# Attention times values: the pair's 128 value columns and a PSUM bank per head, and no clearing product

## The chip, the core and the metric

The kernel runs on one core of a Trainium2 chip. The metric is the device time of one launch in microseconds (us); the median of three runs of the kernel before is 2452.74 us (2452.15 to 2453.5). Engines are named as in the profile: PE (TensorE), DVE (VectorE), ACT (ScalarE), POOL (GpSimd), SP (which issues most of the DMAs).

## The reference, cut to what matters

Two transformer blocks over 512 tokens of 1024 columns, all in float32. Three kinds of attention in them end in a product of a 512 x 512 matrix with 64 value columns for each head:

```
# block 1: softmax attention, 8 MLA heads (masked by chunks of 64) and 8 chunk heads (with a bias)
p = softmax(where(mask, q @ k.T * scale, NEG_INF));            o = p @ v          # v: 512 x 64
# block 2: retention, 8 heads (written with chunks; as one matrix it is causal with decay)
o = (q @ k.T * decay) @ v
# block 2: stick-breaking attention, 8 heads
lneg = where(mask, log_sigmoid(-z), 0); tail = cumsum(lneg, reverse) - lneg
o = where(mask, exp(log_sigmoid(z) + tail), 0) @ v
```

Around them stand dense products (modulation, projections, an MLP) and at the end a mixture of 32 experts, which takes about half of the time.

## The kernel before, in words

All matrices are cut into tiles of 128 rows. A head's attention matrix is held with keys on the partitions and queries along the free dimension, and only the part on and under the diagonal in blocks of 128 is computed: key block `kt` (0 to 3) meets `n = 512 - 128 kt` queries. So a head has four products with its values, of 512, 384, 256 and 128 columns; in each the 128 keys are contracted, the values of that key block are the stationary operand and the attention weights stream. The result is wanted transposed, with the head's 64 value columns on the partitions.

Two heads of even and odd number form a pair. In the kernel before, a pair shares one PSUM bank `po`: the even head's products have its 64 value columns as stationary operand and write partitions 0 to 63, the odd head's write partitions 64 to 127. When both are done, one copy of 128 x 512 takes the bank out. For the softmax and stick-breaking heads the copy is a `split`: ACT writes the rounded part `hh` (line 191) and then DVE the rest `hl` (line 194); for retention it is one ACT copy into `yT` (line 1155).

These operands are plain float32 and not the rounded kind (fp32r) that the dense products use, and every product of float32 operands appears as two MATMULs, each with a weight load of its own.

Three loops issue this work, each as a software pipeline over "units" (head, block), and the order on each engine is the order in which the loop writes it:

- `softmax_attention` (from line 485): step `s` issues the scores of unit `s`, for MLA heads DVE's mask (line 499), the reciprocal of the unit before (line 515), the row maximum (line 501) and ACT's exponential (line 502), for chunk heads DVE's bias and maximum (line 506), the reciprocal, the negation `nm` (line 509) and the exponential (line 510); then DVE's scaling of the unit before (line 520); then, if one is due, the `split` of a finished bank; then the transposes of unit `s - 3` and their copy `pT` (line 562); then the product with the values of unit `s - 9` in `pv`. A split that falls due in step `s` is issued in step `s + 1`, behind the scaling.
- retention in `block2_mix`: scores of unit `s`, DVE's product with the decay into `rw` (line 1141), and the product with the values of unit `s - 3`.
- the stick-breaking loop: scores and a mask product of unit `s`, then Abs, Exp and Ln on ACT (lines 1242 to 1244); DVE turns unit `s - 1` into two parts `sh` and `sl`; PE adds the running sums of unit `s - 3` with the constant matrices in `sc`, and ACT takes the exponential `sw` (line 1268); then the product of unit `s - 5` with the values `vs`.

In the stick-breaking loop a head begins with key block 3, so its first product covers 128 of the 512 columns. A bank is therefore opened by a product with one row of zeros that writes all 128 x 512 elements:

```
if h % 2 == 0 and kt == 3:
    po = self.ps()
    self.mm(po, zero[0:1, :], sc[0:1, 0:4, :].rearrange("p a b -> p (a b)"), True, False)
```

PSUM tiles come from one pool of eight banks.

Of the kernel before, what the change touches and what calls it, by code (L numbers as in the profile page):

```python
# [11 lines left out]
F32R = mybir.dt.float32r  # L12
I32 = mybir.dt.int32
U32 = mybir.dt.uint32
AF = mybir.ActivationFunctionType
OP = mybir.AluOpType
# [113 lines left out]
class Halves:  # L130
    """Eight blocks of columns in two tiles."""

# [8 lines left out]
class Kernel:  # L141
# [36 lines left out]
    def warm(self, n):  # L178
        """Keeps the tensor engine's clock up while it waits for data."""
        if n:  # L180
            ps = self.ps()
            for _ in range(n):
                self.mm(ps[:, 0:P], self.ones, self.ones, True, True)
# [210 lines left out]
    def norm_finish(self, x, xn, ss):  # L394
        """Rows scaled by one over their root mean square."""
        nc = self.nc
        s1 = self.sm.tile([P, NT], F32, name="ns1")
        nc.vector.tensor_tensor(s1, ss[:, :, 0], ss[:, :, 1], op=OP.add)
        r = self.sm.tile([P, NT], F32, name="nr")
        self.rstd(r, s1, D)  # L400
        for t in range(NT):
            if t % 2:
                nc.vector.tensor_scalar(xn[:, t, :], x[:, t, :], r[:, t:t + 1], None, op0=OP.mult)
            else:
                nc.scalar.activation(xn[:, t, :], x[:, t, :], AF.Copy, scale=r[:, t:t + 1])
# [5 lines left out]
    def h_block(self, x, j, scale, bias=None):  # L411
        """One block of columns of x, transposed and scaled, in two parts."""
        nc = self.nc
        ps = self.ps()
        for t in range(NT):
            self.T(ps[:, t * P:(t + 1) * P], x[:, t, j * P:(j + 1) * P])
        if bias is None:
            nc.scalar.activation(self.hh[:, j, :], ps, AF.Copy, scale=scale)  # L418
            nc.vector.scalar_tensor_tensor(self.hl_[:, j, :], ps, scale, self.hh[:, j, :], op0=OP.mult,  # L419
                                           op1=OP.subtract)  # L420
        else:
            tmp = self.junk()
            nc.scalar.activation(tmp, ps, AF.Identity, scale=scale, bias=bias)
            self.split(tmp, self.hh[:, j, :], self.hl_[:, j, :], "dve")

    def h_pair(self, x, j, scale, h, l):
        """As h_block, in tiles of its own."""
        nc = self.nc
        ps = self.ps()
        for t in range(NT):  # L430
            self.T(ps[:, t * P:(t + 1) * P], x[:, t, j * P:(j + 1) * P])
        nc.scalar.activation(h, ps, AF.Copy, scale=scale)
        nc.vector.scalar_tensor_tensor(l, ps, scale, h, op0=OP.mult, op1=OP.subtract)
        return h, l
# [35 lines left out]
    def zeros(self, dst):  # L470
        """Clears what transpose_masked leaves: each head's columns have zeros in the rows of its pair's other one."""
        v = dst.rearrange("p (a b) n -> p a b n", b=2)
        self.nc.gpsimd.memset(v[64:128, :, 0, :], 0.0)
        self.nc.gpsimd.memset(v[0:64, :, 1, :], 0.0)
# [10 lines left out]
    def softmax_attention(self, heads, pool, pool3, tail):  # L485
# [36 lines left out]
        def pv(hd, kt):  # L522
            par = hd["par"]
            if par == 0 and kt == 0:
                self.po = self.ps()
            rows = slice(64 * par, 64 * par + 64)
            self.mm(self.po[rows, kt * P:512], hd["v"](kt), hd["pT"][:, kt, kt * P:512], kt == 0, kt == NT - 1)
            if par == 1 and kt == NT - 1:
                return lambda po=self.po: self.split(po, self.hh[:, hd["pair"], :], self.hl_[:, hd["pair"], :])

# [40 lines left out]
    def block1(self, cg):  # L571
# [19 lines left out]
        with ExitStack() as cx:  # L591
# [44 lines left out]
            def ada(j, m, warm=0):  # L636
                """Columns of the modulation: the first m K tiles on the vector engine."""
                w = wa.pop(j)
# [273 lines left out]
        for h in range(8):  # L912
            heads.append(dict(q=qTm[:, h, :], k=kTm[:, h, :], bias=None, par=h % 2, pair=h // 2,
                              v=lambda kt, h=h: vt[:, kt, h * 64:(h + 1) * 64]))
        for h in range(8):
            heads.append(dict(q=qTc[:, h // 2, :], k=kTc[:, h, :], bias=bias_for(h), par=h % 2,
                              pair=4 + h // 2, v=lambda kt, h=h: vc[:, kt, h * 64:(h + 1) * 64]))
        pso = []
# [122 lines left out]
    def block2_mix(self, right):  # L1041
# [43 lines left out]
        with ExitStack() as cr:  # L1085
# [48 lines left out]
            for s in range(len(units) + la):  # L1134
# [11 lines left out]
                if j >= 0:  # L1146
                    h, kt = units[j]
                    n = 512 - kt * P
                    rows = slice(64 * (h % 2), 64 * (h % 2) + 64)
                    if h % 2 == 0 and kt == 0:  # L1150
                        po = self.ps()
                    self.mm(po[rows, kt * P:512], v[:, kt, h * 64:(h + 1) * 64], wt.pop(j)[:, 0:n], kt == 0,
                            kt == NT - 1)
                    if h % 2 and kt == NT - 1:
                        later = lambda h=h, po=po: nc.scalar.activation(yT[:, h // 2, :], po, AF.Copy)
            later()
# [26 lines left out]
        self.zeros(qTs)  # L1183
        sc = os_.tile([P, 5, P], F32R, name="sc")
        idr, negr, trin, none, zero = [sc[:, i, :] for i in range(5)]
        for i, n in enumerate(("ident", "negm", "trin")):
            nc.vector.tensor_copy(sc[:, i, :], self.cc(n))
        nc.vector.tensor_scalar(none, self.ones, -1.0, None, op0=OP.mult)
        nc.vector.tensor_scalar(zero, self.ones, 0.0, None, op0=OP.mult)
        cs = ExitStack()  # L1190
# [35 lines left out]
        with ExitStack() as cs:  # L1226
# [7 lines left out]
            for s in range(len(units) + la3):  # L1234
# [35 lines left out]
                if 0 <= j < len(units):  # L1270
                    h, kt = units[j]
                    n = 512 - kt * P
                    rows = slice(64 * (h % 2), 64 * (h % 2) + 64)
                    if h % 2 == 0 and kt == 3:
                        po = self.ps()
                        self.mm(po, zero[0:1, :], sc[0:1, 0:4, :].rearrange("p a b -> p (a b)"), True, False)
                    self.mm(po[rows, kt * P:512], vs[:, kt, h * 64:(h + 1) * 64], st.pop(j)[:, 0:n], False, kt == 0)
                    if h % 2 and kt == 0:
                        later[s + 2] = lambda h=h, po=po: self.split(po, self.hh[:, h // 2, :], self.hl_[:, h // 2, :])
        cx.close()  # L1280
# [26 lines left out]
    def router_weights(self):  # L1307
        """Loaded ahead of the router: its weights in two parts and its bias."""
        nc, A, pool = self.nc, self.A, self.big
# [103 lines left out]
    def overflow_blocks(self, rp):  # L1413
        """How many blocks beyond its first each expert has."""
        nc = self.nc
# [5 lines left out]
    def plan(self, rp):  # L1421
        """In steps: which expert's second block shares its weights' pass and the order of the experts that follows
        from it (that expert and TWO change places); the blocks beyond, with their experts, first ranks and places."""
        nc, nb = self.nc, self.nb
# [60 lines left out]
    def swap(self, rp):  # L1485
        """The columns of TWO and of the expert whose second block shares its weights' pass change places."""
        nc = self.nc
# [11 lines left out]
    def gather_onehot(self, d):  # L1499
        """One where a row's number is the token's rank, as the positive part of one less their distance."""  # L1500
        nc = self.nc
# [6 lines left out]
    def gather_table(self, d, a=0, b=2):  # L1508
        """The token (from one) and the gate of each of the block's rows."""
        ps = self.ps()  # L1510
# [6 lines left out]
    def first_rows(self, d, hn):  # L1517
        """The first block's rows, transposed, by products with its one-hot matrix."""
        d["x"] = self.hl_tile("x", d)
# [41 lines left out]
    def m_next(self):  # L1561
        """Parts of the next half chunk (two K tiles); the splits run m_la halves ahead."""
        self.m_ahead()
# [45 lines left out]
    def expert_step(self, cur=(), prev=(), pp=(), nxt=(), extra=None):  # L1609
        """The twelve weight chunks of a step: up products of `cur`'s blocks, down products of `prev`'s, rows of `nxt`'s."""  # L1610
        nc = self.nc
# [112 lines left out]
    def moe_open(self, cx):  # L1724
        """The first expert weights, and the gain of the router's norm."""
        A = self.A
# [14 lines left out]
    def moe_open1(self, cx):  # L1741
        """Ring of expert weights, the biases in two parts and what selects an expert's."""
        nc, A = self.nc, self.A
# [163 lines left out]
    def ple_proj(self, c, pool):  # L1907
        """A half of the columns of p_2 times its projection."""
        ph = self.ph
# [136 lines left out]
```

## Time and profile before

| | |
|---|---|
| median of 3 runs | 2452.74 us |
| span of the profiled execution | 2452.3 us |
| instructions in it | 30624 |
| PE busy | 2419.6 us (99%) |
| DVE busy | 1815.7 us (74%) |
| ACT busy | 1517.4 us (62%) |
| mean granted TensorE clock | 0.991 |

The span runs from the first to the last instruction of one profiled execution. The median of the unprofiled runs lies 0.4 us above it. Busy time of PE counts from the start of a matmul to its modelled end, and matmuls overlap, so 99% does not say that each matmul follows its neighbour at full pace; that is read from start to start. The three attention loops lie at about 170 to 285 us, 797 to 840 us and 915 to 989 us, the experts from about 1180 to 2400 us.

### The profile page before, as it was taken

The page shows a single profiled execution, that of the slowest core. Times are in us where ns is not written, and L with a number is a line of the kernel's source. Part 1 is how long each engine was busy: PE and PEld are TensorE (multiplying, and loading weights), DVE is VectorE, ACT ScalarE, POOL GpSimd, SP SyncE. Part 2 cuts the span into 40 slices and gives each one's busy share as a digit, 9 for nine tenths or more (in the row PEclk, how much of TensorE's full clock was granted, in tenths as well). Part 3 has the DMA queues.
Part 4 walks back from the last instruction along what each step waited for, and adds up shares of the span by engine and source line. Part 5 has one row for each costly group of instructions (what it writes and reads, how often), then busy time and mean ns, then how long its engine had stood idle before and what let it go on. Part 6 is the DMA issues. An engine that isn't in the chain of part 4 may idle for free. (4 is left out here: it accounts for less than half of the span.)

```text
span 2452.3 us, 30624 instructions
## 1 busy us (share of the span) xinstructions
PE 2419.6 (99%) x10796; PEld 1843.8 (75%) x10796; DVE 1815.7 (74%) x2575; ACT 1517.4 (62%) x2201; POOL 164.2 (7%) x108
## 2 busy tenths in 40 slices
PE   8999999999999999989999999999999999999999
PEld 8874688888887475777777777777777777777777
DVE  5876666565556475489888888876888889888874
ACT  3676443334444157467777777855677777777764
POOL 0100000000000000020101010100101010101010
PEclk8999999999999999999999999999999999999999
DMA  9230433342333121579999999877999999999852
GB/s 316 85 126 14 142 105 111 120 121 94 95 113 103 35 68 53 183 259 331 327 335 315 338 321 339 295 254 240 332 337 322 336 321 323 338 326 322 298 190 103
DMA packets 282924, 538.66 MB, mean 220 GB/s; under 512 B 16277, under 2 KB 41397, under 8 KB 282576
## 3 DMA queue, kind: packets, MB, share of 16 engines
q1 hardware_dynamic: 268432, 508.21, 59.6%
q0 software_dynamic: 11792, 26.12, 4.0%
q10 hardware_dynamic: 2544, 2.34, 0.3%
q8 instruction: 86, 1.41, 0.2%
q14 instruction: 70, 0.57, 0.1%
HBM read 530.60 MB, written 23.59 MB: 226 GB/s over the span
## 5 line engine op out<-in xcount | busy, mean ns | idle before, releaser
L194 DVE TENSOR_TENSOR mlo<-mraw,mhi 128x1024 fp32r<-128x1024 f32 x777 | 926.0, 1223 | 181.2 <-ACT mhi L191 173.1
L191 ACT ACTIVATE mhi<-mraw 128x1024 fp32r<-128x1024 f32 x777 | 799.6, 1054 | 203.5 <-PE ps L171 181.6
L171 PE MATMUL ps<-mhi,xh 128*128 128x512 f32 x1024 | 422.7, 413 | 0.0
L171 PE MATMUL ps<-mhi,xl 128*128 128x512 f32 x1024 | 404.4, 395 | 0.0
L171 PE MATMUL ps<-mlo,xh 128*128 128x512 f32 x1024 | 403.6, 394 | 0.0
L171 PEld LDWEIGHTS ps<-mhi,xh 128*128 128x128 f32 x1024 | 192.7, 188 | 67.7 <-issue 30.1
L194 DVE TENSOR_TENSOR wlo<-raw,whi 128x1024 fp32r<-128x1024 f32 (+2 forms) x128 | 152.6, 1203 | 111.2 <-ACT whi L191 110.9
L171 PEld LDWEIGHTS ps<-mhi,xl 128*128 128x128 f32 x1024 | 192.5, 188 | 45.5 <-DVE xl L1596 0.3
L171 PEld LDWEIGHTS ps<-mlo,xh 128*128 128x128 f32 x1024 | 193.1, 189 | 37.3
L191 ACT ACTIVATE whi<-raw 128x1024 fp32r<-128x1024 f32 (+2 forms) x128 | 132.3, 1042 | 131.6 <-PE ps L171 131.2
L171 PE MATMUL ps<-mhi,ah 128*128 128x512 f32 x512 | 211.7, 414 | 0.0
L171 PE MATMUL ps<-mhi,al 128*128 128x512 f32 x512 | 202.3, 395 | 0.0
L171 PE MATMUL ps<-mlo,ah 128*128 128x512 f32 x512 | 202.3, 395 | 0.0
L171 PE MATMUL ps<-whi,hh 128*128 128x512 f32 (+1 forms) x464 | 183.8, 396 | 5.1 <-ACT hh L191 2.4
L171 PE MATMUL ps<-wlo,hh 128*128 128x512 f32 (+1 forms) x464 | 180.8, 390 | 1.9 <-DVE wlo L194 1.9
L171 PE MATMUL ps<-whi,hl 128*128 128x512 f32 (+1 forms) x464 | 180.5, 389 | 0.0
L171 PE MATMUL ps<-hh,whi 128*128 128x512 f32 x352 | 137.8, 392 | 0.0
L171 PE MATMUL ps<-hh,wlo 128*128 128x512 f32 x352 | 137.0, 389 | 0.0
L171 PE MATMUL ps<-hl,whi 128*128 128x512 f32 x352 | 137.0, 389 | 0.0
L1649 ACT ACTIVATE mg<-mg 128x512 f32<-128x512 f32 x66 | 41.7, 632 | 130.2 <-DVE mg L1648 130.2
L171 PEld LDWEIGHTS ps<-mhi,ah 128*128 128x128 f32 x512 | 96.2, 188 | 34.4 <-issue 15.1
L171 PEld LDWEIGHTS ps<-mhi,al 128*128 128x128 f32 x512 | 96.3, 188 | 23.2
(486 smaller groups left out, 3743.1 us busy)
## 6 DMA issues: line engine op xcount, KB each, us to landing
mraw<-in_w_ug SPq DMA_DIRECT2D x256, 1024.0 KB, 6.2
mraw<-in_w_dn SPq DMA_DIRECT2D x128, 1024.0 KB, 6.6
raw<-in_w_up SPq DMA_DIRECT2D x44, 512.0 KB, 3.6
raw<-in_w_in SPq DMA_DIRECT2D x40, 512.0 KB, 3.7
wa<-in_w_ada SPq DMA_DIRECT2D x12, 1024.0 KB, 9.4
raw<-in_w_ada SPq DMA_DIRECT2D x24, 512.0 KB, 4.6
raw<-in_w_down SPq DMA_DIRECT2D x22, 512.0 KB, 3.5
raw<-in_w_out SPq DMA_DIRECT2D x16, 512.0 KB, 4.8
```

The lines of the kernel that those rows point to most:

```text
L171: self.nc.tensor.matmul(out, l, r, start=start, stop=stop, skip_group_check=True)
L191: self.nc.scalar.activation(hi, raw, AF.Copy)
L194: self.nc.vector.tensor_tensor(lo, raw, hi, op=OP.subtract)
L1649: nc.scalar.activation(g, g, AF.Silu, scale=1.702)
```

## The change

All three loops now use the pair's 128 value columns as the stationary operand, for either head. A head's products fill a whole bank of 128 x 512, of which 64 partitions are that head's result and the other 64 are not used; each head has a bank of its own, and only its 64 partitions are copied out, once per head where it was once per pair. In the stick-breaking loop the first product of a head now opens the bank itself, and the product with zeros, its operand and one DVE instruction are gone. Besides, docstrings are emptied, which shifts line numbers by one or two.

```
         def pv(hd, kt):
-            par = hd["par"]
-            if par == 0 and kt == 0:
+            if kt == 0:
                 self.po = self.ps()
-            rows = slice(64 * par, 64 * par + 64)
-            self.mm(self.po[rows, kt * P:512], hd["v"](kt), hd["pT"][:, kt, kt * P:512], kt == 0, kt == NT - 1)
-            if par == 1 and kt == NT - 1:
-                return lambda po=self.po: self.split(po, self.hh[:, hd["pair"], :], self.hl_[:, hd["pair"], :])
+            self.mm(self.po[:, kt * P:512], hd["v"](kt), hd["pT"][:, kt, kt * P:512], kt == 0, kt == NT - 1)
+            if kt == NT - 1:
+                r = slice(64 * hd["par"], 64 * hd["par"] + 64)
+                return lambda po=self.po: self.split(po[r], self.hh[r, hd["pair"], :], self.hl_[r, hd["pair"], :])
...
-                              v=lambda kt, h=h: vt[:, kt, h * 64:(h + 1) * 64]))
+                              v=lambda kt, h=h: vt[:, kt, (h // 2) * P:(h // 2 + 1) * P]))
...
-                    if h % 2 == 0 and kt == 0:
+                    if kt == 0:
                         po = self.ps()
-                    self.mm(po[rows, kt * P:512], v[:, kt, h * 64:(h + 1) * 64], wt.pop(j)[:, 0:n], kt == 0,
+                    self.mm(po[:, kt * P:512], v[:, kt, (h // 2) * P:(h // 2 + 1) * P], wt.pop(j)[:, 0:n], kt == 0,
                             kt == NT - 1)
-                    if h % 2 and kt == NT - 1:
-                        later = lambda h=h, po=po: nc.scalar.activation(yT[:, h // 2, :], po, AF.Copy)
+                    if kt == NT - 1:
+                        later = lambda h=h, po=po, r=r: nc.scalar.activation(yT[r, h // 2, :], po[r], AF.Copy)
...
-                    if h % 2 == 0 and kt == 3:
+                    if kt == 3:
                         po = self.ps()
-                        self.mm(po, zero[0:1, :], sc[0:1, 0:4, :].rearrange("p a b -> p (a b)"), True, False)
-                    self.mm(po[rows, kt * P:512], vs[:, kt, h * 64:(h + 1) * 64], st.pop(j)[:, 0:n], False, kt == 0)
-                    if h % 2 and kt == 0:
-                        later[s + 2] = lambda h=h, po=po: self.split(po, self.hh[:, h // 2, :], self.hl_[:, h // 2, :])
+                    self.mm(po[:, kt * P:512], vs[:, kt, (h // 2) * P:(h // 2 + 1) * P], st.pop(j)[:, 0:n], kt == 3,
+                            kt == 0)
+                    if kt == 0:
+                        later[s + 2] = lambda h=h, po=po, r=r: self.split(po[r], self.hh[r, h // 2, :],
+                                                                          self.hl_[r, h // 2, :])
```

On DVE, in the MLA heads of the softmax loop, these are two steps before (13 and 14, in the fourth head; `nm<-ps` is the row maximum of the step, `prob<-prob,rc` the scaling of the unit before it):

```order
L499 MEMSET ps 64x64
L515 RECIPROCAL rc<-smx 128x1
L501 TENSOR_REDUCE nm<-ps 128x1
L520 TENSOR_SCALAR prob<-prob,rc 128x128
L499 MEMSET ps 64x64
L515 RECIPROCAL rc<-smx 128x1
L501 TENSOR_REDUCE nm<-ps 128x1
L520 TENSOR_SCALAR prob<-prob,rc 128x256
```

And the same steps now:

```order
L499 MEMSET ps 64x64
L515 RECIPROCAL rc<-smx 128x1
L501 TENSOR_REDUCE nm<-ps 128x1
L520 TENSOR_SCALAR prob<-prob,rc 128x128
L194 TENSOR_TENSOR hl<-ps,hh 64x512
L499 MEMSET ps 64x64
L515 RECIPROCAL rc<-smx 128x1
L501 TENSOR_REDUCE nm<-ps 128x1
L520 TENSOR_SCALAR prob<-prob,rc 128x256
```

The subtraction `hl` of a split stands between the scaling of a 128-column unit and the mask of the next step in every head from the fourth on; before, it stood there in every second head, from the fifth on.

On PE, in the stick-breaking loop, this is how the first bank was opened before (`sh`, `sl` with `sc` are the running sums, `sw,vs` the product with the values, `qTs,kTs` the next scores):

```order
L171 MATMUL ps<-sh_7481,sc 128x384
L171 MATMUL ps<-sl_7482,sc 128x384
L171 MATMUL ps<-sc 128x512
L171 MATMUL ps<-sw,vs 64x128
L171 MATMUL ps<-qTs,kTs 128x384
```

And now:

```order
L171 MATMUL ps<-sh_7512,sc 128x384
L171 MATMUL ps<-sl_7513,sc 128x384
L171 MATMUL ps<-sw,vs 128x128
L171 MATMUL ps<-qTs,kTs 128x384
```

The product with zeros is gone, in four places in all, and the products with the values write 128 partitions where they wrote 64; the order of all other products of PE is kept in the three loops.

## Rows read from the trace of the kernel before

**Rows 1.** Stretches: us, then busy PE, PEld, DVE, ACT, POOL, clock, DMA, GB/s
```profile
165.00:181.00 16.00, 12.89 (x58) 8.78 (x57) 8.77 (x36) 11.18 (x31) 1.08 (x2) 0.79 0.36 128
181.00:284.00 103.00, 103.00 (x400) 49.69 (x399) 64.25 (x279) 59.68 (x179) 3.39 (x7) 1.00 0.10 32
...
798.00:838.00 40.00, 40.00 (x114) 13.81 (x113) 13.88 (x29) 1.79 (x3) 0.00 (x0) 1.00 0.00 1
...
939.09:975.29 36.20, 36.20 (x163) 21.40 (x162) 21.46 (x51) 27.77 (x66) 0.00 (x0) 1.00 0.00 1
...
1180.00:2400.00 1220.00, 1217.29 (x5297) 926.79 (x5295) 1032.77 (x1108) 899.59 (x1095) 115.15 (x64) 1.00 0.89 310
```

**Rows 2.** Timeline of PE, one softmax step: start, duration, operation, out<-in, shape, count
```profile
234.31 0.49 PE L187 MATMUL ps<-cst,prob 128*128 128x128 f32 x3
234.73 1.07 PE L171 MATMUL ps<-pT,x 128*64 128x512 f32 x2
235.73 0.91 PE L171 MATMUL ps<-kTc,qTc 128*128 128x384 f32 x2
236.48 0.60 PE L187 MATMUL ps<-cst,prob 128*128 128x128 f32 x4
```

**Rows 3.** Timeline of PE, scores behind transposes without a product with values between
```profile
172.53 0.60 PE L171 MATMUL ps<-kTm,qTm 128*128 128x256 f32 x2
...
172.75 0.38 PE L171 MATMUL ps<-kTm,qTm 128*128 128x256 f32 x1
```

**Rows 4.** Timeline of PE, the last seven products with values of the softmax loop
```profile
281.70 3.12 PE L171 MATMUL ps<-pT,x 128*64 128x384 f32 x14
```

**Rows 5.** Timeline of DVE, an MLA head with a split (square brackets: idle before, releaser)
```profile
194.39 0.41 DVE L501 TENSOR_REDUCE nm<-ps 128x1 f32<-128x256 f32 x1
...
195.97 0.69 DVE L194 TENSOR_TENSOR hl<-ps,hh 128x512 fp32r<-128x512 f32 x1 [0.98 <-ACT hh L191]
...
196.81 0.56 DVE L501 TENSOR_REDUCE nm<-ps 128x1 f32<-128x384 f32 x1
...
198.54 0.69 DVE L501 TENSOR_REDUCE nm<-ps 128x1 f32<-128x512 f32 x1
...
201.16 0.41 DVE L501 TENSOR_REDUCE nm<-ps 128x1 f32<-128x256 f32 x1
```

**Rows 6.** Timeline of ACT in that head: the exponential's sums of the 384-column step
```profile
197.95 0.19 ACT L502 ACTIVATION_READ_ACCUMULATOR prob<-ps,nm 128x1 f32 x1
```

**Rows 7.** Timeline of DVE, a chunk head with a split
```profile
235.08 0.15 DVE L509 TENSOR_SCALAR nm<-mx 128x1 f32<-128x1 f32 x1
...
236.44 0.69 DVE L194 TENSOR_TENSOR hl<-ps,hh 128x512 fp32r<-128x512 f32 x1 [1.00 <-ACT hh L191]
...
237.64 0.15 DVE L509 TENSOR_SCALAR nm<-mx 128x1 f32<-128x1 f32 x1
...
238.96 0.69 DVE L506 CUSTOM_DVE_ANT_0 prob<-ps,relb 128x512 f32<-128x512 f32 x1 [0.89 <-PE ps L171]
...
239.69 0.15 DVE L509 TENSOR_SCALAR nm<-mx 128x1 f32<-128x1 f32 x1
...
240.87 0.14 DVE L509 TENSOR_SCALAR nm<-mx 128x1 f32<-128x1 f32 x1
...
241.85 0.15 DVE L509 TENSOR_SCALAR nm<-mx 128x1 f32<-128x1 f32 x1
```

**Rows 8.** ACT copies of 512 columns from PSUM: duration min/median/max in ns
```profile
L191 ACT ACTIVATE hh<-ps x7: 575/576/606, 195.4 to 280.2; 128x512 fp32r<-128x512 f32 x7
```

**Rows 9.** The same for copies of 64 partitions
```profile
L482 ACT ACTIVATE qT<-ps x8: 590/592/595, 768.7 to 773.0; 64x512 f32<-64x512 f32 x8
```

**Rows 10.** Costliest groups of the page: DVE's part of a weight chunk's split
```profile
L194 DVE TENSOR_TENSOR wlo<-raw,whi 128x1024 fp32r<-128x1024 f32 (+2 forms) x128 | 152.6, 1203 | 111.2 <-ACT whi L191 110.9
```

**Rows 11.** Timeline of PE, the stick-breaking loop around a product with zeros
```profile
940.33 0.49 PE L171 MATMUL ps<-sc 1*128 1x512 f32 x1
940.75 0.43 PE L171 MATMUL ps<-sw,vs 128*64 128x128 f32 x2
```

More of the change, by code (lines that the diff above doesn't have):

```diff
@@ L913, in block1 @@
             heads.append(dict(q=qTm[:, h, :], k=kTm[:, h, :], bias=None, par=h % 2, pair=h // 2,
-                              v=lambda kt, h=h: vt[:, kt, h * 64:(h + 1) * 64]))
+                              v=lambda kt, h=h: vt[:, kt, (h // 2) * P:(h // 2 + 1) * P]))
         for h in range(8):
             heads.append(dict(q=qTc[:, h // 2, :], k=kTc[:, h, :], bias=bias_for(h), par=h % 2,
-                              pair=4 + h // 2, v=lambda kt, h=h: vc[:, kt, h * 64:(h + 1) * 64]))
+                              pair=4 + h // 2, v=lambda kt, h=h: vc[:, kt, (h // 2) * P:(h // 2 + 1) * P]))
         pso = []
@@ L1148, in block2_mix @@
                     n = 512 - kt * P
-                    rows = slice(64 * (h % 2), 64 * (h % 2) + 64)
-                    if h % 2 == 0 and kt == 0:
+                    r = slice(64 * (h % 2), 64 * (h % 2) + 64)
+                    if kt == 0:
                         po = self.ps()
-                    self.mm(po[rows, kt * P:512], v[:, kt, h * 64:(h + 1) * 64], wt.pop(j)[:, 0:n], kt == 0,
+                    self.mm(po[:, kt * P:512], v[:, kt, (h // 2) * P:(h // 2 + 1) * P], wt.pop(j)[:, 0:n], kt == 0,
                             kt == NT - 1)
-                    if h % 2 and kt == NT - 1:
-                        later = lambda h=h, po=po: nc.scalar.activation(yT[:, h // 2, :], po, AF.Copy)
+                    if kt == NT - 1:
+                        later = lambda h=h, po=po, r=r: nc.scalar.activation(yT[r, h // 2, :], po[r], AF.Copy)
             later()
@@ L1183, in block2_mix @@
         self.zeros(qTs)
-        sc = os_.tile([P, 5, P], F32R, name="sc")
-        idr, negr, trin, none, zero = [sc[:, i, :] for i in range(5)]
+        sc = os_.tile([P, 4, P], F32R, name="sc")
+        idr, negr, trin, none = [sc[:, i, :] for i in range(4)]
         for i, n in enumerate(("ident", "negm", "trin")):
@@ L1188, in block2_mix @@
         nc.vector.tensor_scalar(none, self.ones, -1.0, None, op0=OP.mult)
-        nc.vector.tensor_scalar(zero, self.ones, 0.0, None, op0=OP.mult)
         cs = ExitStack()
@@ L1272, in block2_mix @@
                     n = 512 - kt * P
-                    rows = slice(64 * (h % 2), 64 * (h % 2) + 64)
-                    if h % 2 == 0 and kt == 3:
+                    r = slice(64 * (h % 2), 64 * (h % 2) + 64)
+                    if kt == 3:
                         po = self.ps()
-                        self.mm(po, zero[0:1, :], sc[0:1, 0:4, :].rearrange("p a b -> p (a b)"), True, False)
-                    self.mm(po[rows, kt * P:512], vs[:, kt, h * 64:(h + 1) * 64], st.pop(j)[:, 0:n], False, kt == 0)
-                    if h % 2 and kt == 0:
-                        later[s + 2] = lambda h=h, po=po: self.split(po, self.hh[:, h // 2, :], self.hl_[:, h // 2, :])
+                    self.mm(po[:, kt * P:512], vs[:, kt, (h // 2) * P:(h // 2 + 1) * P], st.pop(j)[:, 0:n], kt == 3,
[3 more added lines that the diff above has]
+                                                                          self.hl_[r, h // 2, :])
         cx.close()
```

## The prediction

> **What bounds the kernel now.** I first read the stretches. In the softmax loop PE is busy 103.00 of 103.00 us, in retention 40.00 of 40.00, in four heads of the stick-breaking loop 36.20 of 36.20, while DVE and ACT are busy 4 to 77% of the time; among the experts it is 1217 of 1220 us [rows 1]. So PE sets the end in every stage the change touches, and the experts, also PE's, will simply start earlier by whatever the loops give: their DMA share of 0.89 leaves the loads behind PE, not ahead of it. A busy PE need not be at full pace, however, and that I read next, from start to start.
>
> Three transposes last 0.49 us and four 0.60 [rows 2], so one costs 0.11 at full pace. Scores of 256 columns, which like the products with values are two MATMULs, start 0.22 us apart when transposes stand before them (172.53, 172.75) [rows 3]; so a pass takes 0.22 us per 256 columns, 0.32 for 384, 0.43 for 512. Against this, one softmax step [rows 2]: transposes at 234.31, the product with values at 234.73: 0.42, where three transposes take 0.33. From it to the scores 1.00, where two passes take 0.86. From the scores to the next transposes 0.75, where two passes take 0.64. So each product with 64 value columns costs 0.09 + 0.14 + 0.11 = 0.34 us beyond its columns, around it and in the product behind it. The scores behind transposes in rows 3 do not pay it: it comes with the 64-column shape.
>
> One thing speaks against the change. The last seven products with values of the softmax loop, 14 passes over 4096 columns, run 3.12 us from first start to last end [rows 4]; at the pace above they would need 4096 / 256 x 0.22 = 3.5. Two heads overlap there by some 0.5 us, which the change loses. [...]
>
> **The change part by part.** *The switch.* 64 + 32 + 32 products. The new ones have the same shape of weights as scores and transposes, so I take the 0.34 as gone for each that stands between other shapes. Nothing is added for columns: a pass streams as many as before. The weight load doubles, 128 columns for 64; for scores behind transposes such a load hides in the matmul before [rows 3], and I cost it at nothing; uncovered it would be bounded by the part that the first pass now pays after a switch, 0.1 us.
>
> *Retention.* 28 products lie between scores, four stand together at the end: 28 x 0.34 + 0.3 = 9.8 us; DVE, 13.88 us busy in 40, hides the rest, and four more ACT copies fall on an engine that is busy 1.79 us of 40 [rows 1]. 10 us saved.
>
> *Softmax.* Here PE alone would save 54 x 0.34 + 0.9 - 0.5 = 18.8 us. But half a bank costs the copying engine as much as a whole one: ACT copies of 64 x 512 take 592 ns [rows 9], of 128 x 512 576 [rows 8]. There are 16 splits where there were 8, and a split stands in DVE's queue ahead of the next step's mask, reciprocal and maximum, which the next exponential needs. So I follow the chain DVE, ACT, DVE through a head with a split and leave out where it waits for PE. MLA head, from maximum to maximum [rows 5]: 256 to 384 columns 2.42 us (hl waits 0.98 for hh, then 0.69); 384 to 512 is 1.73 with a wait for PE; without it ACT's sums are ready at 197.95 + 0.19 = 198.14 [rows 6], and 0.1 later the maximum could start, so 1.44; 512 over 128 to 256 2.62. Sum 6.48. The head takes 201.16 - 194.39 = 6.77 now, and PE after the change 6.77 - 4 x 0.34 = 5.4. So the chain takes PE's place: an MLA head saves 0.29, not 1.36. Chunk head, from nm to nm [rows 7]: 2.56 with the split, 2.05 less the 0.89 of waiting for PE, 1.18, 0.98: 5.88; it saves 0.89. The loop has steps 9 to 63 with products behind them: 9 to 12 without a split save PE's 1.4; the other 4.75 MLA heads 1.4; eight chunk heads 7.1; the tail, with PE alone, 0.9 - 0.5. From this goes one weight chunk that DVE splits near the end and that PE's lag now covers: its DVE part is 1.2 us [rows 10]; I take 1.5 with ACT's wait. Sum 8.8; since PE can run ahead of the chain only as far as eight banks allow, which no row prices, I bound that between nothing and the 8.5 that the heads give, and take 0.8: 8 us.
>
> *Stick-breaking.* A product with zeros goes: 0.42 us from its start to the next [rows 11], four of them, 1.7. With 28 x 0.34 and 0.9 at the ends PE saves 12.1. A head takes 36.20 / 4 = 9.05 now and would take 9.05 - 1.36 - 0.21 = 7.48. ACT is busy 27.77 / 4 = 6.94 per head [rows 1] and gets half a copy more, 0.29: 7.23. PE remains the longest, by 3%. Two engines so close, in queues that wait for each other, lose something: between nothing (12.1) and all but the zeros' 1.7; I take a head at 7.7, near PE's value because the loop has two to three steps of slack between them. That loses 0.2 x 7 heads; the first two heads fill the pipeline and are ACT's anyway, 0.9 less: 9.8 us. DVE, 21.46 of 36.20 us, gets eight subtractions for four and keeps room.
>
> *Smaller.* One DVE instruction on 128 columns before the loop goes, off the path. No DMA moves; the queues of SP and POOL hold the same rows.
>
> Sum: 8 + 10 + 9.8 = 27.8 us. The profiled span is 2452.3, and the median lies 0.4 above it, so the forecast is 2452.7 - 27.8 = 2425.
>
> **The rivals.** *PE alone counts.* If the splits hide (PE so far ahead that each chain's stall is made up elsewhere), all of 18.8 + 9.8 + 12.1 = 41 us is saved: 2412. For it: PE is the only engine that is full. Against it: the chain is a loop through two engines, each link waits for the one before, and its 6.48 us leaves nothing to make up.
>
> *The chains take nearly all.* If the softmax loop stays at its 6.77 (banks held by waiting splits), and stick-breaking at ACT's pace with 1 us lost per head at hand-overs, retention's 10, 1.7 for the zeros and some 2.5 at the ends remain: 14 us, 2439. For it: the MLA chain is within 5% of today's pace. Against it: DVE waits for PE up to 0.89 us per step even in a head with a split [rows 7].
>
> [...]
>
> *The switch does not go.* If the 0.34 us comes from something other than the shape, say from the change of operands, all of it stays, the first load grows by up to 0.05, 128 x 0.05 = 6.4, and the zeros give 1.7 back: 2457. Rows 3 speak against it: scores with new operands behind transposes pay nothing.
>
> **How the numbers follow.** The forecast has 0.62, with a range of its own of 2418 to 2433 (softmax 3 to 12, stick-breaking 7 to 12). PE alone 0.15, the chains 0.17, the clock 0.03, the switch 0.03. A difference of 0.2%, 4.9 us, is about what a measurement of this kernel can tell from no change. Faster by more than that: the first three, less 0.01 for chains that take still more, 0.93; within it 0.03; slower 0.04. The range is 2411 to 2440: it takes in most of the first two rivals and leaves out the last two and the far ends, about 0.15.
>
> **What would show it.** In the profile after: products with values are 128 columns wide, and their two passes start 0.43 us apart for 512 columns; scores behind them start their passes at the same pace. Retention shrinks to some 30 us per seven heads. In an MLA head a split stands in every head, the period is near 6.5, PE idles about 1 us in it, and the releaser of that idle is ACT or DVE; in a chunk head it is near 5.9. In stick-breaking the period of a pair falls from 18.1 to about 15.4. Wrong would be: MLA heads at 5.4 (the chain is no loop), a clock below 1 in the loops, or a time among the experts that changes by more than a few us, since nothing there is touched.

## The result and the profile after

The changed kernel takes 2428.6 us (median of 4 runs, 2427.3 to 2429.7), the kernel before 2453.1 us in the same job: a ratio of 0.990 (95% interval 0.988 to 0.991), 24.5 us less. The forecast was 27.8 less, 2425, with a range of 2411 to 2440. The mechanism held in each of the three loops; the 3 us that are missing were lost 1400 us behind the last of them.

The profiled span went from 2452.3 to 2427.6 us. To see where, I matched PE's matmuls of the two traces one by one and took by how much each starts earlier:

| | forecast | measured | earlier by, at its end |
|---|---|---|---|
| ahead of the loops (nothing changed there) | 0 | 0.5 | 0.5 |
| softmax loop | 8 | 8.3 | 8.8 |
| retention | 10 | 9.9 | 18.7 |
| stick-breaking | 9.8 | 9.4 | 28.2 |
| output projection to the last expert | 0 | -0.2 | 28.0 |
| the branch behind the experts and what follows | 0 | -3.2 | 24.7 |

Stretches of the profile after, placed to answer [rows 1] (us; busy PE, PEld, DVE, ACT, POOL; granted clock, DMA share, GB/s):

```profile
180.00:275.00 95.00, 89.47 (x400) 56.95 (x400) 70.04 (x289) 64.26 (x188) 3.22 (x6) 1.00 0.11 31
790.00:820.00 30.00, 30.00 (x114) 19.00 (x113) 13.76 (x28) 4.14 (x7) 0.00 (x0) 1.00 0.00 1
915.80:946.66 30.86, 30.79 (x161) 23.49 (x160) 22.64 (x53) 28.82 (x69) 0.00 (x0) 1.00 0.00 1
1152.00:2361.00 1209.00, 1208.61 (x5264) 920.59 (x5263) 1027.80 (x1104) 892.53 (x1085) 116.08 (x64) 1.00 0.90 311
```

The same 400 matmuls of the softmax loop now lie in 95 us, with PE idle for 5.5 of them, where it had been busy throughout; 114 of retention lie in 30 us for 40; four stick-breaking heads in 30.86 for 36.20. The clock stays at 1.00 in all three: it did not fall, for which the prediction had a chance of 0.03.

PE in one softmax step, answering [rows 2] (start, duration, operation):

```profile
229.61 0.55 PE L187 MATMUL ps<-cst,prob 128*128 128x128 f32 x3
230.00 1.02 PE L171 MATMUL ps<-pT,x 128*128 128x512 f32 x2
230.86 0.81 PE L171 MATMUL ps<-kTc,qTc 128*128 128x384 f32 x2
231.50 0.60 PE L187 MATMUL ps<-cst,prob 128*128 128x128 f32 x4
231.94 0.81 PE L171 MATMUL ps<-pT,x 128*128 128x384 f32 x2
```

From the product with values to the scores it is 0.86 us (1.00 before), from these to the transposes 0.64 (0.75): two passes at 0.43 and 0.32, nothing on top. The four transposes behind take 0.44, 0.11 each. So the 0.14, the 0.11 and the 0.09 of the prediction went with the 64-column shape; what in PE makes that shape cost them no run here shows.

The last seven products with values, answering [rows 4]:

```profile
272.54 3.62 PE L171 MATMUL ps<-pT,x 128*128 128x384 f32 x14
```

3.62 us for 3.12: the overlap of two heads in the tail was there, 0.5 us by modelled ends as predicted; to the start of the product behind it is 3.38 for 3.06, so 0.3 of it was lost. This 3.12 for 3.62 is all that was seen of an overlap of 64-column products, and only there, where products of two heads stand next to each other.

DVE in two MLA heads, answering [rows 5], and in a pair of chunk heads, answering [rows 7] (square brackets: idle before, releaser):

```profile
194.55 0.69 DVE L194 TENSOR_TENSOR hl<-ps,hh 64x512 fp32r<-64x512 f32 x1 [1.11 <-ACT hh L191]
...
195.59 0.56 DVE L501 TENSOR_REDUCE nm<-ps 128x1 f32<-128x384 f32 x1
...
197.03 0.67 DVE L501 TENSOR_REDUCE nm<-ps 128x1 f32<-128x512 f32 x1
...
199.62 0.40 DVE L501 TENSOR_REDUCE nm<-ps 128x1 f32<-128x256 f32 x1
...
202.03 0.56 DVE L501 TENSOR_REDUCE nm<-ps 128x1 f32<-128x384 f32 x1
...
206.06 0.40 DVE L501 TENSOR_REDUCE nm<-ps 128x1 f32<-128x256 f32 x1
...
207.77 0.69 DVE L194 TENSOR_TENSOR hl<-ps,hh 64x512 fp32r<-64x512 f32 x1 [1.11 <-ACT hh L191]
...
208.82 0.56 DVE L501 TENSOR_REDUCE nm<-ps 128x1 f32<-128x384 f32 x1
...
227.95 0.15 DVE L509 TENSOR_SCALAR nm<-mx 128x1 f32<-128x1 f32 x1
...
239.80 0.15 DVE L509 TENSOR_SCALAR nm<-mx 128x1 f32<-128x1 f32 x1
```

From 384 to 512 columns 1.44 us (forecast 1.44), to 256 columns 2.59 (2.62), from there over the split 2.41 (2.42): 6.44 for this MLA head where 6.48 was forecast. The next one takes 6.79 (202.03 to 208.82), with 2.76 over its split (206.06 to 208.82). The two alternate, so an MLA head takes 6.61 on average (194.55 to 207.77, from split to split over two heads). It took 6.77 before. The chunk heads take 11.85 / 2 = 5.93 (5.88). None is at PE's 5.4.

What waited in 180 to 214 us (who, for whom: us, times, longest):

```profile
ACT prob L502 <- DVE nm L501: 11.2, 22, 1.2
DVE rc L515 <- ACT prob L502: 4.7, 11, 0.5
DVE hl L194 <- ACT hh L191: 4.2, 4, 1.1
PEld ps L187 <- ACT pT L561: 4.2, 6, 0.9
PE ps L187 <- DVE ps L499: 3.1, 6, 0.6
```

DVE and ACT wait for each other and PE for both: the chain took PE's place, as argued.

Starts of four stick-breaking heads (scores of 128 columns), and the product with values ahead of the first:

```profile
922.85 0.86 PE L171 MATMUL ps<-sw,vs 128*128 128x384 f32 x2
923.54 0.39 PE L171 MATMUL ps<-qTs,kTs 128*128 128x128 f32 x2
...
931.34 0.39 PE L171 MATMUL ps<-qTs,kTs 128*128 128x128 f32 x2
...
938.87 0.39 PE L171 MATMUL ps<-qTs,kTs 128*128 128x128 f32 x2
...
946.66 0.39 PE L171 MATMUL ps<-qTs,kTs 128*128 128x128 f32 x2
```

7.80, 7.53, 7.79: 7.7 on average, as forecast; 7.5 is PE's own pace. The product of 384 columns at 922.85 takes 0.69 to the next start, 0.05 over its two passes; so does its like in the other heads of the loop.

Now the loss. PE behind the last expert, before:

```profile
2389.17 0.39 PE L171 MATMUL ps<-mhi,mraw 128*128 128x512 f32 x1
2391.87 1.22 PE L171 MATMUL ps<-mraw 128*128 128x512 f32 x2 [2.31 <-issue]
```

and after:

```profile
2361.17 0.39 PE L171 MATMUL ps<-mhi,mraw 128*128 128x512 f32 x1
2366.92 0.79 PE L171 MATMUL ps<-mraw 128*128 128x512 f32 x1 [5.35 <-DVE mlo L194]
```

Start to start 2.70 us became 5.74. Between the two stands the loop over extra experts (L1862 before, L1861 after), which runs zero times here. The profile puts the wait down to a subtraction of DVE that ended shortly before; but before the change PE went on with DVE idle in the whole pause (the stretches below), so PE doesn't need it. The instructions of that line on PE's sequencer (count, then ns min/median/max) tell more, before:

```profile
L1862 PEldq COMPARE_BRANCH  x3: 97/187/333, 2386.6 to 2391.6; - x3
```

and after:

```profile
L1861 PEldq COMPARE_BRANCH  x3: 97/193/3360, 2358.7 to 2366.7; - x3
```

One branch takes 3360 ns for 333, and that is the whole 3.0. Into it falls a transfer of instructions: the trace's records of queue 8 show one that starts at 2362.90, 1.0 us after the start of the branch, and takes 0.97. The page has this queue as

```profile
q8 instruction: 86, 1.41, 0.2%
```

86 packets of 16.4 KB, one for every 253 of PE's 21769 records, and about evenly spaced so all through the run (between two starts PE passes 255 records in the median): I take it, by these counts alone, for the queue by which PE's program comes in. The rest of the 3.2, 0.2 us, goes with the clock. Stretches around the pause, before:

```profile
2389.00:2392.00 3.00, 0.69 (x4) 0.26 (x2) 0.00 (x0) 0.60 (x2) 0.00 (x0) 0.97 0.12 15
2392.00:2402.00 10.00, 9.55 (x37) 7.39 (x38) 6.04 (x6) 8.38 (x14) 0.00 (x0) 0.84 0.98 344
```

and after:

```profile
2361.00:2367.00 6.00, 0.65 (x4) 0.22 (x2) 1.91 (x2) 3.59 (x5) 0.00 (x0) 0.74 0.45 159
2367.00:2377.00 10.00, 9.56 (x36) 7.39 (x37) 4.07 (x5) 5.25 (x10) 0.00 (x0) 0.81 0.88 328
```

The stretch with the longer pause has a granted clock of 0.74 for 0.97 (0.50 from 2364 to 2367 us), and the first 10 us behind it have 0.81 for 0.84. From the next matmul to the end it is 60.64 us for 60.44. Over all the kernels below this end follows the clock of its first 10 us (taken from that matmul on): 60.44 to 60.52 us at 0.83, 61.06 at 0.77. It is not the pause alone that sets it: three kernels with the long pause have 0.83 too, and 60.45 to 60.48.

### The profile page after: what moved, and what is told of

It reads as the page before. It is cut to its first block, busy times and chain, and to the rows that moved or that the text cites. A ratio compares the mean times of both kernels' runs of the same rounds, so it can differ in the third digit from the quotient of the medians.

```text
span 2427.6 us, 30631 instructions
## 1 busy us (share of the span) xinstructions
PE 2385.8 (98%) x10792; PEld 1861.6 (77%) x10792; DVE 1821.8 (75%) x2586; ACT 1525.8 (63%) x2217; POOL 165.1 (7%) x108
```

## Experiments

Three questions: is it the shape, and nothing else of the change, that gives the gain; is it the split's stall in DVE's queue that holds the softmax heads above PE's pace; and what makes the branch longer. All ratios are to the kernel before, run on the same chip in the same job.

**The shape alone.** The changed kernel, with a bank and a copy per head and without the product with zeros, but with 64 value columns again in all three loops (here the softmax loop):

```diff
-            self.mm(self.po[:, kt * P:512], hd["v"](kt), hd["pT"][:, kt, kt * P:512], kt == 0, kt == NT - 1)
+            r = slice(64 * hd["par"], 64 * hd["par"] + 64)
+            self.mm(self.po[r, kt * P:512], hd["v"](kt), hd["pT"][:, kt, kt * P:512], kt == 0, kt == NT - 1)
...
-                              v=lambda kt, h=h: vt[:, kt, (h // 2) * P:(h // 2 + 1) * P]))
+                              v=lambda kt, h=h: vt[:, kt, h * 64:(h + 1) * 64]))
```

> One part alone, in all three loops: a bank and a copy per head and no product with zeros, but the head's own 64 value columns as stationary operand. Theory A (the 0.34 us per product comes with the 64-column shape; the chain through a split takes 6.48 us and hides behind PE's 6.77): heads of the softmax loop stay at 6.77 us, of retention at 5.7, of stick-breaking at 8.84 (9.05 without the zeros); only the zeros' 1.7 us are saved: 2451 us, ratio 0.999. Theory B (two heads sharing a bank cost the time): a head of the softmax loop near 6.4 or below, retention near 4.3; about 2428, ratio 0.990.

Measured: 2454.7 us, ratio 1.000 (0.999 to 1.001). Its softmax step:

```profile
234.31 0.91 PE L171 MATMUL ps<-kTc,qTc 128*128 128x384 f32 x2
235.06 0.60 PE L187 MATMUL ps<-cst,prob 128*128 128x128 f32 x4
235.59 0.86 PE L171 MATMUL ps<-pT,x 128*64 128x384 f32 x2
```

0.75 from the scores to the transposes again, and 0.53 for four transposes whose pace needs 0.44: the 0.11 and 0.09 are back. Heads take 6.77 (softmax), 5.68 (retention) and 8.84 us (stick-breaking, the zeros' 0.21 per head gone), by the starts of their scores. So but for the zeros' 1.7 all that the loops gave came with the 128-column shape. More banks and twice as many copies gave nothing, and cost nothing as long as PE, at its old pace, hid them. At the last expert PE was 2.8 us ahead of the kernel before, behind the branch 0.2 late: the pause is 5.71 us in this kernel too, which has the zero products no longer, but the old shape. So the pause doesn't come from being 28 us earlier.

**Retention alone.** The kernel before, with only the retention's products and copies changed:

```diff
...
-                    self.mm(po[rows, kt * P:512], v[:, kt, h * 64:(h + 1) * 64], wt.pop(j)[:, 0:n], kt == 0,
+                    self.mm(po[:, kt * P:512], v[:, kt, (h // 2) * P:(h // 2 + 1) * P], wt.pop(j)[:, 0:n], kt == 0,
...
-                    if h % 2 and kt == NT - 1:
-                        later = lambda h=h, po=po: nc.scalar.activation(yT[:, h // 2, :], po, AF.Copy)
+                    if kt == NT - 1:
+                        later = lambda h=h, po=po, r=r: nc.scalar.activation(yT[r, h // 2, :], po[r], AF.Copy)
```

> The kernel before with the change in retention alone, where no chain of other engines is long. Theory A: a retention head goes from 5.67 to 4.3 us, 9.9 us in all, and all of it arrives at the end: 2443 us, ratio 0.996. Theory B (the experts' loads, not PE, set the later stages): the head is as short, but the time stays within 3 us of before, ratio 0.999 or more.

Measured: 2442.7 us, ratio 0.995 (0.994 to 0.997), 10.6 us less by the medians. A head, from 512 columns to 512 columns:

```profile
800.00 1.02 PE L171 MATMUL ps<-rw,rv 128*128 128x512 f32 x2
...
804.32 1.02 PE L171 MATMUL ps<-rw,rv 128*128 128x512 f32 x2
```

4.32 us for 5.68, four times 0.34. With PE alone in the way and the zero products still there, the gain of the loop arrives undiminished at the end, and the pause at the branch is 2.70.

**The row maximum ahead of the reciprocal.** The changed kernel, with the MLA step's reciprocal (which waits for ACT's sums) behind the maximum in DVE's queue:

```diff
-                mid()
                 nc.vector.tensor_reduce(out=nm, in_=ps[:, 0:n], axis=AX.X, op=OP.max, negate=True)
+                mid()
```

> The changed kernel, but in MLA heads DVE takes the row maximum ahead of the reciprocal of the unit before, so that the maximum no longer waits for the exponential before it. Theory A (the chain DVE, ACT, DVE sets the MLA heads): their period falls from 6.45 us to about 5.5, near PE's 5.4; 4.75 heads times 0.9 give 4 us: 2424 against 2428.6 of the changed kernel, ratio 0.988. Theory B (the eight banks, or PE itself, hold the MLA heads at 6.45): the period stays above 6.2 and the time within 1.5 us of the changed kernel. Chunk heads stay at 5.93 under both.

Measured: 2426.8 us, ratio 0.989 (0.988 to 0.991). The expectation of 5.5 us per MLA head missed; it takes 6.17, from split to split, for 6.61 in the changed kernel (the 6.45 of the expectation was the shorter of two heads that alternate):

```profile
192.65 0.69 DVE L194 TENSOR_TENSOR hl<-ps,hh 64x512 fp32r<-64x512 f32 x1 [0.92 <-ACT hh L191]
...
198.82 0.68 DVE L194 TENSOR_TENSOR hl<-ps,hh 64x512 fp32r<-64x512 f32 x1 [0.78 <-ACT hh L191]
```

That is 0.44 per head, some 2 us over 4.75 heads. The time is 1.8 less than the changed kernel's, which its interval doesn't tell apart, and it falls between the two theories. The maximum's wait was one link; the other, the subtraction that stalls DVE for ACT's copy, stayed.

**The low half one step later.** The changed kernel, with the copy (ACT) where it was and the subtraction (DVE) one step on, when the copy is long done:

```diff
-                return lambda po=self.po: self.split(po[r], self.hh[r, hd["pair"], :], self.hl_[r, hd["pair"], :])
+                def hi(po=self.po):
+                    h = self.hh[r, hd["pair"], :]
+                    nc.scalar.activation(h, po[r], AF.Copy)
+                    return lambda: nc.vector.tensor_tensor(self.hl_[r, hd["pair"], :], po[r], h, op=OP.subtract)
+                return hi
...
+            if low:
+                low()
+                low = None
             if later:
-                later()
+                low = later()
```

> The changed kernel, but in the softmax loop DVE's subtraction hl of a split is issued one step after ACT's hh, so that DVE does not wait for hh with the next maximum behind it. Theory A (the split's stall in DVE's queue is what the chain has over PE): chunk heads go from 5.93 us to 5.5 or less, MLA heads from 6.45 to about 6.0; 8 x 0.45 + 4.75 x 0.5 = 6 us less than the changed kernel: 2422.5, ratio 0.9875. Theory B (the waits of PE in this loop come from banks that unsplit heads hold): holding a bank a step longer makes both periods equal or longer, 2428 to 2432.

Measured: 2421.8 us, ratio 0.987 (0.985 to 0.988), 6.8 less than the changed kernel. DVE in two heads:

```profile
193.69 0.69 DVE L531 TENSOR_TENSOR hl<-ps,hh 64x512 fp32r<-64x512 f32 x1
...
199.24 0.67 DVE L531 TENSOR_TENSOR hl<-ps,hh 64x512 fp32r<-64x512 f32 x1
...
204.69 0.69 DVE L531 TENSOR_TENSOR hl<-ps,hh 64x512 fp32r<-64x512 f32 x1
```

No wait stands ahead of it any more, and the heads, MLA and chunk alike, take 5.4 to 5.6 us, PE's pace, though a bank is now held a step longer. So taking away the split's stall is enough to bring the softmax heads to PE's pace, and it isn't the banks that held them above it. The loop ends 9.3 us earlier than in the changed kernel, of which PE has 7.9 left at the experts: waits for other things in the output projection and the routing take the rest.

**Eight more instructions on PE.** The changed kernel, with two more of the products on ones that stand ahead of the experts, where PE waits for data anyway. They replace the eight instructions that went with the zero products:

```diff
-        self.warm(24)
+        self.warm(26)
```

> Edit: the changed kernel with two more float32 products on ones (eight PE instructions) in the run of 24 that stands between the output projection and the experts, where PE waits for data anyway; nothing else. It is about the pause of PE behind the experts, at the branch into the loop over extra blocks: 2.70 us in the kernel before, 5.74 in the changed one. Theory C: the pause depends on how many instructions PE's stream has ahead of the branch (the four zero products that went were eight), so eight more bring it back: pause 2.7 us, time 2428.6 - 3 = 2425.6. Rival: the pause comes from how loads or other engines stand to PE there, 28 us earlier than before: pause 5.7, time 2428.6 or up to 1 more.

Measured: 2426.7 us, ratio 0.989 (0.987 to 0.991), and

```profile
L1861 PEldq COMPARE_BRANCH  x3: 97/187/421, 2357.3 to 2362.3; - x3
```

The branch is short again and the pause 2.78 us. The time is 1.9 less; by its interval alone it isn't told apart from the changed kernel's, by the branch it is.

**Four more.** The same with 25 products.

> Edit: as the run with eight more PE instructions, but with one product, four instructions. Theory C: the pause at the branch is one of the two values, 2.7 or 5.7 us, or lies between if it goes by the distance left to read; a single look. Rival (timing of loads or other engines): 5.7 as in the changed kernel.

Measured: 2429.0 us (one run), pause 5.88: one of the two values, nothing between.

**Low half later and eight more instructions.** Both edits at once.

> Edit: the changed kernel with the low half of the split one step later and eight more PE instructions. If the two gains are apart (6.8 from the low half, 3 from the pause): 2421.8 - 3 = 2418.8, pause 2.7. If the pause goes by timing: 2421.8, pause 5.7.

Measured: 2419.9 us, ratio 0.986 (0.984 to 0.988), 1.9 below the low half alone, which the intervals don't tell apart. But the pause is 6.08 us, and the branch

```profile
L1870 PEldq COMPARE_BRANCH  x3: 97/193/3700, 2348.9 to 2357.2; - x3
```

The number of matmuls (10796, as in the kernel before) doesn't decide then. Besides its products and weight loads, this kernel has 173 instructions in PE's stream, nearly all of them semaphores, though, where the one with the short branch has 185 and the kernel before 195: the order of the engines' waits changes how many of these are needed.

**Stick-breaking with DVE's copy.** The same kernel, with the high half of the stick-breaking split made by DVE instead of ACT:

```diff
-                                                                          self.hl_[r, h // 2, :])
+                                                                          self.hl_[r, h // 2, :], "dve")
```

> Edit: as the run with low half later and eight more PE instructions, and in the stick-breaking attention DVE instead of ACT makes the high half of the split (a copy per head, four in all of each kind go from ACT to DVE). Theory S: a stick-breaking head takes 7.7 where PE alone needs 7.5 because ACT, 94% busy, is late at hand-overs; with ACT relieved it takes 7.5: 8 x 0.2 = about 1.5 us less than that run. Rival: DVE's queue, in which the split now stands twice, is later and the head takes 7.7 or more: same or up to 2 us longer.

Measured: 2419.8 us, ratio 0.986 (0.984 to 0.987), so no difference in the time; but the heads start at

```profile
906.89 0.39 PE L171 MATMUL ps<-qTs,kTs 128*128 128x128 f32 x2
...
914.41 0.38 PE L171 MATMUL ps<-qTs,kTs 128*128 128x128 f32 x2
...
921.94 0.38 PE L171 MATMUL ps<-qTs,kTs 128*128 128x128 f32 x2
```

every 7.53 us, PE's pace, where without the edit they alternate around 7.7. The loop took 62.0 us from its first scores to its last product for 63.7. ACT's lateness was the 0.2 per head, as theory S had it. That the 1.7 aren't seen in the time stays open: in this profile PE reached the softmax loop 1.7 us later than without the edit, and 0.9 went between the stick-breaking loop and the end.

**Where the branch stands, tried from both sides.** The last kernel with 30 products on ones, so that its place in the stream passes the limit which the runs so far leave:

```diff
-        self.warm(26)
+        self.warm(30)
```

> Edit: as the run with the low half later and the stick-breaking high half on DVE, with 30 products on ones in place of 26 (16 more PE instructions). The run with eight more instructions and the low half later paused 6.08 us at the branch, though it has as many matmuls as the one that paused 2.78: theory C as first put (number of matmuls) has failed. Theory D: the place of the branch in PE's whole stream decides, its semaphore instructions among them. By the trace's records the next matmul behind the branch is number 21239, 21239, 21229 where the pause was 2.7 to 2.8, and 21209 to 21225 where it was 5.7 to 6.1; here it will be 21233: pause 2.7 to 2.8, time 2419.8 - 3.3 = 2416.5. Rival (timing of loads and other engines, 37 us earlier than before): pause 5.7 to 6.1, time 2420.

Measured: 2416.4 us, ratio 0.985 (0.983 to 0.987); pause 2.73 us, and

```profile
L1870 PEldq COMPARE_BRANCH  x3: 97/190/327, 2347.9 to 2352.9; - x3
```

This is the fastest kernel of the study: 3.4 less than the same with 26 products, in another job and with intervals that overlap, but with a pause that is 3.3 shorter. And the kernel before, with 20 products for 24:

> Edit: the kernel before, with 20 products on ones in place of 24 (16 fewer PE instructions), nothing else; the next matmul behind the branch is number 21223. Theory D: the pause at the branch grows from 2.70 to 5.7 us and the time by 3, to about 2456, in a kernel that is nowhere earlier than before. Rival (timing, the 28 us): pause 2.7, time 2453.

Measured: 2457.2 us (one run; the kernel before 2453.6 in that job), pause 5.92 us, and

```profile
L1862 PEldq COMPARE_BRANCH  x3: 97/187/3441, 2386.2 to 2394.4; - x3
```

All kernels, sorted by how many instructions PE's stream has up to the matmul behind the branch (counted in the trace, semaphore and branch instructions among them):

| kernel | place | pause, us |
|---|---|---|
| low half later | 21209 | 5.73 |
| low half later, 8 more | 21217 | 6.08 |
| the same, stick-breaking copy on DVE | 21217 | 6.04 |
| changed | 21221 | 5.74 |
| shape alone | 21221 | 5.71 |
| maximum ahead of the reciprocal | 21222 | 5.81 |
| before, 16 fewer | 21223 | 5.92 |
| changed, 4 more | 21225 | 5.88 |
| changed, 8 more | 21229 | 2.78 |
| stick-breaking copy on DVE, 24 more | 21233 | 2.73 |
| before | 21239 | 2.70 |
| retention alone | 21239 | 2.70 |

Twelve kernels, one limit between 21225 and 21229, and two groups of pauses, 2.7 to 2.8 us and 5.7 to 6.1. The last two runs were built to cross the limit, one in either direction, and did. So the number of instructions in PE's stream decides. That timing does is refuted: the kernel before with 16 fewer gets the long pause though it is only 0.5 us earlier at the last expert, and the changed kernel with eight more has the short one 29 us earlier. Not told apart are the place of the branch and the length of the whole stream: all the edits stand ahead of the branch, and behind the count of the table each kernel has the same 548 records. The instruction transfers stand differently to the branch in the two groups. In the kernels with the short pause the last one ahead of the branch starts 3.9 to 8.5 us before the last expert matmul (8.5 in the kernel before); in those with the long pause it starts 33 to 34 us before it (33.5 in the changed kernel), and the next comes only within the long branch. From this I read it as the place of the branch among these transfers, and take the long branch to wait for one. Both are my reading and not shown: that the branch needed that transfer no record says, and why it takes 3.36 to 3.70 us where the transfer in the changed kernel took 0.97 stays open.

## Why the prediction was right, and where it was not

*PE sets the end in every stage, the 0.34 us go with the 64-column shape.* Right. Steps run at 0.43 and 0.32 us per pass, retention heads take four times 0.34 less, and with 64 columns put back every head is back at its old pace. The rival that the switch does not go is refuted by that pair.

*Softmax: the chain takes PE's place.* Right in mechanism, and in size partly by luck. By PE's lead over the kernel before, steps 9 to 12 gave 1.3 us (forecast 1.4), the MLA heads behind them 1.7 (1.4), the chunk heads with the tail 5.3 (5.2 by the terms of the sum; the 1.5 for the weight chunk and the 0.8 for the banks in it no run prices by themselves). The middle term came right by luck. MLA heads take 6.44 and 6.79 in turn, so the 6.48, followed through one head, fits every other one, and a head saves 0.16 on average where the sum had 0.29; but the first of these heads still ran near PE's pace and gave 1.1 at once. Chunk heads take 5.93 (5.88). The rival of PE alone has this loop wrong for this kernel, and nearly right with one subtraction a step later: then heads run at 5.4, and the loop gives 17.6 of the 18.8. It was the stall in DVE's queue, behind which the next maximum stands, and not the work of eight more splits.

*Retention.* 9.9 for 10.

*Stick-breaking.* A head of 7.7 for 7.7; the loop 9.4 for 9.8. The head behind the first, where the pipeline still fills, takes 8.05 (scores start at 900.06 and 908.12; 9.10 before), and that is most of the 0.4. ACT was indeed the engine that is late: with one copy per head taken from it the heads run at 7.53. The rival of chains that take nearly all came near for the MLA heads alone (6.61 for 6.77); the chunk heads at 5.93 and the stick-breaking heads at 7.7 refute it.

*Twice the weight load, at nothing.* Right but for 0.05 us at such a place as 922.85, behind a product of 128 columns, once per stick-breaking head; that it is the weight load which shows there is not shown. A load took 136 ns (median) for 64 columns and takes 189 to 191 for 128.

*"The experts, also PE's, will simply start earlier by whatever the loops give."* This is the step that failed, by 3.2 of 27.8 us. It holds to the last expert, 28.0 us earlier. Then PE's branch takes 3.36 us for 0.33, because the change takes eight instructions (the zero products) and ten semaphore instructions out of PE's program, and this took it over a limit. The prediction counted instructions by their time only, not by their number ahead of the branch. With eight instructions put back, the changed kernel was 27.2 us faster than the kernel before in its job (2426.7 for 2453.9).

## What to carry to other kernels

Where one engine is full in every stage, follow the next chain through the queues before taking its gain: here it was one subtraction that stood in a queue ahead of what the other engines needed, and moving it one step on gave 6.8 us on top of the change's 24.5. And a gain that is smaller at the end than in its stage is found by matching the instructions of two traces one by one: the place where the lead drops is the place to look at, however far from the edit.

## What was not expected of the hardware

In the lines above, PE's branch behind the experts took 0.33 to 0.42 us or 3.36 to 3.70, by how many instructions PE's stream has ahead of it, with a limit that four instructions cross. Four products on ones (16 instructions) more or fewer, in a place where PE waits, moved the whole kernel by 3.4 us (across two jobs) and 3.6 (one run). So instructions that cost no time where they run can cost or save it elsewhere, and semaphore instructions, whose number follows from the order of the work, count in it. An experiment that adds or removes a few instructions ahead of a run-time loop should be read with that branch's duration beside it: the kernel with the old shape was 2.8 us ahead at the last expert, and its time showed none of it.
